# The state space's gate projection by halves of the features, four first halves taken during the scan

## The chip, the cores and the metric

The kernel runs on one core of one Trainium2 chip. The metric is the time of one execution on the device in microseconds (us). The kernel before takes 2056.19 us, the median of three runs (2054.28 to 2064.1). Engines have short names in the profile: PE multiplies matrices, PEld loads its weights, DVE is the vector engine, ACT the scalar engine, POOL is GpSimd, and SP issues most DMAs. A name that ends in q is that engine's queue.

## The reference, cut to what matters

Two transformer-like blocks are computed for 256 tokens of 1024 features. The change touches one place near the end, the second half of `s5_mixer` (a state space model with 64 groups):

```python
u = h @ w_in                                     # 1024 x 1024
s_r, s_i = associative_scan(...)                 # over the 256 tokens
y = einsum(s_r, c_re) - einsum(s_i, c_im) + d_skip * u
y = gelu(y)                                      # 256 tokens x 1024 features
ya, yb = split(y @ w_glu, 2)                     # w_glu is 1024 x 2048
return ya * sigmoid(yb)                          # 256 x 1024, then x = x + g1 * that
```

The last product is the gate projection. Each output feature needs all 1024 features of `y`. Everything is float32.

## The kernel before, in words

**Weights and their parts.** A weight matrix arrives as a stream of tiles of 128 x 2048 floats (1 MB each), issued on SP into four raw buffers. `Parts.split` (lines 131 to 149) cuts each tile into two parts of 128 x 1024, and each part into `hi`, a rounded copy that ACT makes (line 145), and `lo`, the remainder that DVE makes (line 146, `lo = w - hi`). There are four buffers for such parts. `Parts.get` hands out the next part, and sees that two more are split ahead of it. A part holds eight blocks of 128 x 128. `three` (lines 240 to 249) multiplies one block in three matmuls: `hi` with the high part of the activations (line 247), `hi` with the low part (line 248), `lo` with the high part (line 249), all added in one PSUM bank.

**The scan.** The features lie in eight chunks of 128. For c = 0 to 7, `rotated_inputs(c + 1)` multiplies on PE (line 1755), `scan(c)` does nine instructions and two more into the state `S` on DVE (lines 1766 to 1779), and `from_states(c)` multiplies the states on PE (lines 1790 and 1792) into a bank `c` that two values of c share. `load` issues the scan's tables on POOL's queue (line 1744), three chunks ahead. `fill` puts matrix-vector products of another layer's modulation between these steps (line 225, whose weights POOL's queue loads too, line 113, and whose ends are lines 229 to 237). `gelu` follows for each pair of chunks (ACT 1799, DVE 1800, ACT 1801, DVE 1804), and `outputs(half)` puts four chunks back into feature order (sixteen copies on ACT and DVE, line 1722) and makes their high and low parts `hh` and `hl` (ACT 1725, DVE 1726). `outputs(0)` is called at c = 5, and `outputs(1)` behind the loop.

**The gate projection.** Behind the loop, for each of eight output chunks d, `chunks8` is called for `ya` and for `yb` (one part, eight blocks, 24 matmuls each, k over all eight feature chunks), both into one bank of the pool of four that `rotated_inputs` uses as well. ACT's sigmoid (line 1852) and four further ACT and DVE instructions follow (lines 1853 to 1855, 1447, 1448).

**The order.** The text of the kernel is not the order of the engines. A planner orders each engine's instructions ahead of time: among those that it takes to be ready, the one written first goes first, and those marked with a low priority later. Each engine then works strictly in that order. An instruction may so stand ahead of others that were written before it: 24 matmuls of the first gate chunk stand between the scan's last matmuls, though they are written behind the loop.

Of the kernel before, what the change touches and what calls it, by code (L numbers as in the profile page):

```python
# [8 lines left out]
F32 = mybir.dt.float32  # L9
# [4 lines left out]
ALU = mybir.AluOpType  # L14
# [38 lines left out]
def bc(ap, dim, n):  # L53

    a = list(ap.ap)
    a.insert(dim, [0, n])
    return bass.AP(tensor=ap.tensor, offset=ap.offset, ap=a)
# [64 lines left out]
class Parts:  # L122
# [3 lines left out]
    def __init__(self, nc, stream, pool):  # L126
        self.nc, self.stream, self.pool = nc, stream, pool
        self.at, self.made, self.ready, self.whole = 0, {}, 0, set()

    def split(self, n):  # L130

        st = self.stream
        while self.ready < n:
            i, h = divmod(self.ready, 2)
            if h == 0:
                st.issue(i)
                self.raw = st.tiles.pop(i)
            w = self.raw[:, h * 1024:(h + 1) * 1024]
            if self.ready in self.whole:
                self.made[self.ready] = (w,)  # L140
                self.ready += 1
                continue
            parts = self.pool.tile([128, self.stream.width], F32, tag="w", name="parts").bitcast(F32R)
            hi, lo = parts[:, :1024], parts[:, 1024:]
            self.nc.scalar.copy(out=hi, in_=w)  # L145
            self.nc.vector.tensor_tensor(out=lo, in0=w, in1=hi.bitcast(F32), op=ALU.subtract)  # L146
            self.made[self.ready] = (hi, lo)
            self.ready += 1

# [91 lines left out]
def three(pe, o, w, j, a, k, first, last):  # L241

    sl = slice(j * 128, (j + 1) * 128)
    if len(w) == 1:
        pe.matmul(out=o, lhsT=w[0][:, sl], rhs=a[0][:, k], start=first, stop=last)
        return
    pe.matmul(out=o, lhsT=w[0][:, sl], rhs=a[0][:, k], start=first, stop=False)  # L247
    pe.matmul(out=o, lhsT=w[0][:, sl], rhs=a[1][:, k], start=False, stop=False)  # L248
    pe.matmul(out=o, lhsT=w[1][:, sl], rhs=a[0][:, k], start=False, stop=last)  # L249
# [1112 lines left out]
def second_block(tc, g, out):  # L1362
    nc, A, ws, ada = tc.nc, g.A, g.ws, g.ada
    v, s, pe = nc.vector, nc.scalar, nc.tensor
# [8 lines left out]
    def bank(name="b"):  # L1373
        return psb.tile([128, 512], F32, tag="b", name=name)

    def core_bank(name="c"):
        return psc.tile([128, 512], F32, tag="c", name=name)

    def small_bank(name="s"):
        return pss.tile([128, 512], F32, tag="s", name=name)  # L1380
# [28 lines left out]
    hh = b2.tile([128, 8, 256], F32R, name="h2h")  # L1409
    hl = b2.tile([128, 8, 256], F32R, name="h2l")  # L1410
# [57 lines left out]
    def chunks8(o, a):  # L1468

        w = ws.get()  # L1470
        for k in range(8):
            three(pe, o, w, k, a, k, k == 0, k == 7)
# [12 lines left out]
    for k in range(0, 8, 2):  # L1485
        b = bank()
# [7 lines left out]
    b = small_bank()  # L1494
# [3 lines left out]
    b = b[:, :4].rearrange("p (t n) -> p n t", t=2)  # L1498
# [81 lines left out]
    with ExitStack() as er:  # L1580
# [26 lines left out]
        for h in range(4):  # L1607
            q = rotated("q", 0 if h == 0 else None)
            k = rotated("k", 2 if h == 0 else None)
# [8 lines left out]
            b = core_bank()  # L1618
# [7 lines left out]
            st = r2.tile([128, 2, 6], F32, tag="st", name="st")  # L1626
# [17 lines left out]
            for t in range(2):  # L1644
# [3 lines left out]
                b = core_bank()  # L1648
# [3 lines left out]
                d = (slice(None), slice(4 * h, 4 * h + 4), slice(t * 128, (t + 1) * 128))  # L1652
# [35 lines left out]
    with ExitStack() as e5:  # L1688
# [70 lines left out]
        def scan(c):  # L1759
            b, m = rot.pop(c)  # L1760
            E = loaded.pop((1, c))
            Ec, Es = (E[:, i].rearrange("p q j -> p (q j)") for i in range(2))
            b3 = b.rearrange("p (i x) -> p i x", i=2)
            t1 = q5.tile([128, 2, 256], F32, tag="t1", name="t1")
            t2 = q5.tile([128, 2, 256], F32, tag="t2", name="t2")
            v.tensor_tensor(out=t1, in0=b3, in1=bc(Ec, 1, 2), op=ALU.mult)
            v.tensor_tensor(out=t2, in0=b3, in1=bc(Es, 1, 2), op=ALU.mult)
            z = q5.tile([128, 2, 256], F32, tag="z", name="z", bufs=1)
            v.tensor_tensor(out=t1[:, 0], in0=t1[:, 0], in1=t2[:, 1], op=ALU.add)
            v.tensor_tensor(out=t1[:, 1], in0=t1[:, 1], in1=t2[:, 0], op=ALU.subtract)  # L1770
            for i in range(2):
                v.tensor_tensor_scan(out=z[:, i], data0=m, data1=t1[:, i], initial=0.0, op0=ALU.mult, op1=ALU.add)
            v.tensor_tensor(out=t1, in0=z, in1=bc(Ec, 1, 2), op=ALU.mult)
            v.tensor_tensor(out=t2, in0=z, in1=bc(Es, 1, 2), op=ALU.mult)

            S = states[c % 2]
            t1q, t2q = (t.rearrange("p i (q j) -> p i q j", q=4)[:, :, :, :63] for t in (t1, t2))
            v.tensor_tensor(out=S[:, 0, :, 1:], in0=t1q[:, 0], in1=t2q[:, 1], op=ALU.subtract)
            v.tensor_tensor(out=S[:, 1, :, 1:], in0=t2q[:, 0], in1=t1q[:, 1], op=ALU.add)
            load(1, c + 3)  # L1780

        def from_states(c):
            o2, S = loaded.pop((2, c)), states[c % 2]
            CA = [o2[:, 640 * i:640 * i + 640].rearrange("p (q n) -> p q n", q=4) for i in range(2)]
            T = o2[:, 1280:].rearrange("p (q n) -> p q n", q=4)
            if c % 2 == 0:
                yb[c // 2] = core_bank()
            for q in range(4):
                yo = yb[c // 2][:, (c % 2 * 4 + q) * 64:(c % 2 * 4 + q) * 64 + 64]
                pe.matmul(out=yo, lhsT=T[:, q], rhs=U[:, 4 * c + q], start=True, stop=False)  # L1790
                for i in range(2):
                    pe.matmul(out=yo, lhsT=CA[i][:, q, 32:], rhs=S[:, i, q], start=False, stop=(i == 1))  # L1792
            load(2, c + 3)
# [26 lines left out]
        def fill(i):  # L1820
            while at[0] < FILL[i]:
                ada.part(small_bank, p5)
                at[0] += 1

        for c in range(8):
            if c < 7:
                rotated_inputs(c + 1)
            scan(c)
            fill(2 * c)
            if c % 2 == 0 and c >= 2:  # L1830
                gelu(c // 2 - 1, False)
            if c % 2 == 1 and c >= 3:
                gelu(c // 2 - 1, True)
                if c == 5:
                    outputs(0)
            from_states(c)
            fill(2 * c + 1)
        gelu(3, False)
        gelu(3, True)
# [5 lines left out]
        sc, sh = mod[:, 24:32], mod[:, 32:40]  # L1845
        early, sq, sums, then = next_norm(sc, sh)
        for d in range(8):
            b = bank()
            chunks8(b[:, :256], (hh, hl))
            chunks8(b[:, 256:], (hh, hl))  # L1850
            sg = q5.tile([128, 256], F32, tag="sg", name="sg")
            s.activation(out=sg, in_=b[:, 256:], func=ACTF.Sigmoid)
            v.tensor_tensor(out=sg, in0=b[:, :256], in1=sg, op=ALU.mult)
            v.scalar_tensor_tensor(out=xT[:, d], in0=sg, scalar=mod[:, 16 + d:17 + d], in1=xT[:, d], op0=ALU.mult, op1=ALU.add)
            s.activation(out=sq[:, d], in_=xT[:, d], func=ACTF.Square)
            then(d)
# [16 lines left out]
    b = ffn(1, early, R, between1, last1)  # L1873
# [5 lines left out]
    for t in range(2):  # L1879
        for h in range(2):  # L1880
            b = bank()
# [12 lines left out]
def tile_body(ctx, tc, A, out):  # L1894
    nc = tc.nc
    g = Ctx()
# [4 lines left out]
    st = Stream(nc, wst, NSTAGE, 2048)  # L1901
# [36 lines left out]
    for l in range(2):  # L1938
        st.add([A["ffn_up"][l, i] for i in range(22)])
        st.add([A["ffn_down"][l, i] for i in range(11)])  # L1940
        if l == 0:
            st.add([A["s5_w_in"][i] for i in range(4)])
            st.add([A["s5_glu"][i] for i in range(8)])

    pvt = cst.tile([128, A["pvec"].shape[1]], F32, name="pvt")
# [39 lines left out]
    with ExitStack() as es:  # L1985
# [7 lines left out]
        leftovers(tc, g)  # L1993
        es_mw.close()
    second_block(tc, g, out)


def host_arrays(inputs):
# [14 lines left out]
    I = {k: np.asarray(a) for k, a in inputs.items()}  # L2013
    d = {}
# [38 lines left out]
    def blocks(w, order):  # L2053

        K, N = w.shape
        t = w.reshape(K // 128, 128, N // 128, 128).transpose(2, 0, 1, 3)[order]
        return t.reshape(-1, 16, 128, 128).transpose(0, 2, 1, 3).reshape(-1, 128, 2048)
# [3 lines left out]
    d["ret_w_out"] = blocks(I["ret_w_out_2"][0], np.arange(8))  # L2061
    d["w_o"] = blocks(np.concatenate([wg, wo[512:]], axis=0), np.arange(8))
    d["s5_w_in"] = blocks(I["s5_w_in_2"][0], np.arange(8))
    d["s5_glu"] = blocks(I["s5_w_glu_2"][0], np.arange(16).reshape(2, 8).T.reshape(-1))
    d["ffn_up"] = np.stack([blocks(w, np.arange(44).reshape(2, 22).T.reshape(-1)) for w in I["ffn_w_up_2"]])
    d["ffn_down"] = np.stack([blocks(w, np.arange(8)) for w in I["ffn_w_down_2"]])

# [10 lines left out]
    c, s = np.cos(ang).astype(f), np.sin(ang).astype(f)  # L2078
# [28 lines left out]
```

## Time and profile before

| | |
|---|---|
| median of three runs | 2056.19 us |
| the profiled execution, its own time | 2056.63 us |
| its span, first to last instruction | 2054.9 us |
| PE busy | 1931.3 us (94%) |
| DVE busy | 1107.8 us (54%) |
| ACT busy | 649.8 us (32%) |
| POOL busy | 59.4 us (3%) |
| mean granted TensorE clock | 0.979 of 2.4 GHz |

The busy times are averages over stages that differ. The change lies in the stage from about 1724 us (the scan's start) to about 1850 us (the end of the gate projection). Times inside it are counted from the span's start. The granted clock is 1.00 at 2.4 GHz and 0.50 at 1.2 GHz.

### The profile page before, as it was taken

The numbers are of one execution on the slowest core, as the hardware profiler recorded it, in microseconds if no ns is written. First come the engines' busy times: TensorE is split into PE (matmuls) and PEld (weight loads), VectorE is DVE, ScalarE is ACT, GpSimd is POOL, SyncE is SP. The second block draws the span as 40 slices with busy tenths as digits, with TensorE's granted clock in tenths as the row PEclk, the third lists the DMA queues.
The fourth block names the chain that finished last, engine by engine and source line by source line (L and its number), as shares of the span: only waits on it lengthen the run. The fifth ranks groups of instructions, "written<-read, shape, count | busy, mean of one in ns | idle before, by whom it ended". The sixth has DMA issues, their size and how long they took to land. (4 is left out here: it accounts for less than half of the span.)

```text
span 2054.9 us, 28954 instructions
## 1 busy us (share of the span) xinstructions
PE 1931.3 (94%) x11162; PEld 1244.0 (61%) x11162; DVE 1107.8 (54%) x2364; ACT 649.8 (32%) x1134; POOL 59.4 (3%) x92
## 2 busy tenths in 40 slices
PE   6999989999899999999999979999999999799998
PEld 4756844333233333343333327888999999599998
DVE  3856654322122122132222228998898879869863
ACT  5455211000000000010000014445677646346542
POOL 1000010000000000000000000000101002100000
PEclk9999989999999999999999998999999999899999
DMA  8657659999999999999999994667857688655641
GB/s 335 224 199 278 243 193 413 421 421 421 421 422 421 421 421 421 421 421 401 421 421 421 421 374 156 215 230 275 284 213 257 251 290 301 237 181 189 225 182 62
DMA packets 101757, 643.40 MB, mean 313 GB/s; under 512 B 11584, under 2 KB 12880, under 8 KB 34288
## 3 DMA queue, kind: packets, MB, share of 16 engines
q1 hardware_dynamic: 94176, 613.46, 76.0%
q0 software_dynamic: 6624, 26.76, 3.8%
q8 instruction: 89, 1.46, 0.3%
q10 hardware_dynamic: 816, 1.30, 0.2%
q14 instruction: 52, 0.43, 0.1%
HBM read 626.79 MB, written 14.68 MB: 312 GB/s over the span
## 5 line engine op out<-in xcount | busy, mean ns | idle before, releaser
L914 PE MATMUL hc<-w,xe 128*64 128x512 f32 (+1 forms) x2008 | 470.5, 596 | 38.8 <-DMA w<-in_w_in_dram 38.7
L914 PEld LDWEIGHTS hc<-w,xe 128*64 128x64 f32 (+1 forms) x2008 | 144.6, 138 | 350.0 <-issue 234.7
L146 DVE TENSOR_TENSOR parts<-w,parts 128x1024 fp32r<-128x1024 f32 x238 | 289.3, 1219 | 57.1 <-ACT parts L145 55.5
L145 ACT CAST parts<-w 128x1024 fp32r<-128x1024 f32 x238 | 248.7, 1048 | 192.8 <-PE b L249 115.3
L247 PE MATMUL b<-h2h,parts 128*128 128x256 f32 x896 | 255.7, 286 | 10.3 <-ACT h2h L1725 9.1
L248 PE MATMUL b<-h2l,parts 128*128 128x256 f32 x896 | 255.7, 286 | 0.4 <-DVE h2l L1429 0.2
L249 PE MATMUL b<-h2h,parts 128*128 128x256 f32 x896 | 254.1, 284 | 0.0
L914 PE MATMUL yb<-w,hb 128*64 128x512 f32 (+1 forms) x1024 | 252.7, 603 | 0.8 <-DMA w<-in_w_out_dram 0.8
L934 DVE COPY hs<-hc 128x512 f32<-128x512 f32 x33 | 22.8, 691 | 417.4 <-PE hc L914 417.4
L247 PEld LDWEIGHTS b<-h2h,parts 128*128 128x128 f32 x896 | 170.5, 191 | 12.7 <-ACT h2h L1725 9.3
L248 PEld LDWEIGHTS b<-h2l,parts 128*128 128x128 f32 x896 | 170.5, 190 | 4.2 <-issue 1.3
L249 PEld LDWEIGHTS b<-h2h,parts 128*128 128x128 f32 x896 | 170.4, 190 | 0.2 <-issue 0.2
L932 ACT COPY hs<-hc 128x512 f32<-128x512 f32 x33 | 19.3, 585 | 437.0 <-PE hc L914 437.0
L914 PEld LDWEIGHTS yb<-w,hb 128*64 128x64 f32 (+1 forms) x1024 | 67.4, 138 | 129.5 <-issue 118.6
L199 DVE SCALAR_TENSOR_TENSOR acc<-w,c,acc 128x1024 f32<-128x1024 f32 x77 | 98.4, 1278 | 19.4 <-DMA w<-in_ada_w_dram 19.4
L247 PE MATMUL b<-ah,parts 128*128 128x256 f32 x352 | 100.3, 285 | 1.9 <-DVE xT L264 1.7
L249 PE MATMUL b<-ah,parts 128*128 128x256 f32 x352 | 99.8, 283 | 0.1
L248 PE MATMUL b<-al,parts 128*128 128x256 f32 x352 | 99.1, 282 | 0.0
L977 ACT COPY ys<-yb 64x512 f32<-64x512 f32 (+1 forms) x32 | 18.5, 579 | 236.1 <-PE yb L914 224.6
L896 PEld LDWEIGHTS gb<-S,h 128*128 128x128 f32 x544 | 66.5, 197 | 37.2 <-issue 26.6
L1527 PE MATMUL b<-parts,h2h 128*128 128x512 f32 x256 | 82.4, 401 | 0.9 <-DVE parts L146 0.6
L1005 DVE TENSOR_TENSOR yacc<-sc,yacc 128x512 f32<-128x512 f32 x68 | 46.6, 688 | 66.8 <-PE sc L1003 66.8
(517 smaller groups left out, 2971.6 us busy)
## 6 DMA issues: line engine op xcount, KB each, us to landing
w<-in_w_in_dram SPq DMA_DIRECT2D x252, 1024.0 KB, 19.8
w<-in_w_out_dram SPq DMA_DIRECT2D x128, 1024.0 KB, 19.8
w<-in_ffn_up_dram SPq DMA_DIRECT2D x44, 1024.0 KB, 4.9
w<-in_ada_w_dram SPq DMA_DIRECT2D x72, 512.0 KB, 5.2
w<-in_ret_w_in_dram SPq DMA_DIRECT2D x24, 1024.0 KB, 5.0
w<-in_ffn_down_dram SPq DMA_DIRECT2D x22, 1024.0 KB, 4.8
w<-in_w_ada_dram SPq DMA_DIRECT2D x32, 512.0 KB, 3.9
w<-in_ada_w_dram POOLq DMA_DIRECT2D x24, 512.0 KB, 4.7
```

Source lines behind the costliest of these rows:

```text
L145: self.nc.scalar.copy(out=hi, in_=w)
L146: self.nc.vector.tensor_tensor(out=lo, in0=w, in1=hi.bitcast(F32), op=ALU.subtract)
L199: v.scalar_tensor_tensor(out=self.acc, in0=w, scalar=cc, in1=self.acc, op0=ALU.mult, op1=ALU.add)
L247: pe.matmul(out=o, lhsT=w[0][:, sl], rhs=a[0][:, k], start=first, stop=False)
L248: pe.matmul(out=o, lhsT=w[0][:, sl], rhs=a[1][:, k], start=False, stop=False)
L249: pe.matmul(out=o, lhsT=w[1][:, sl], rhs=a[0][:, k], start=False, stop=last)
L896: g.got = pe.matmul(out=b[:, k * 128:k * 128 + n], lhsT=g.h2[:, t, d * 128:(d + 1) * 128], rhs=S[:, t, :n], start=(t == 0), stop=(t == 1))
L914: g.got = pe.matmul(out=on, lhsT=x, rhs=w[:, n * 512:n * 512 + 512], start=first, stop=last)
L932: s.copy(out=h, in_=hc[e][n])
L934: v.tensor_copy(out=h, in_=hc[e][n])
L1005: v.tensor_tensor(out=y, in0=b, in1=y, op=ALU.add)
L1527: pe.matmul(out=bs[t], lhsT=x[:, kk, tsl], rhs=y[:, k * 512:(k + 1) * 512], start=(kk == 0 and i == 0), stop=(kk == 7 and i == 2))
```

## The change

Each part of the gate's weights now holds, for one output chunk, the blocks of four feature chunks for `ya` and `yb` (2 x 4 blocks in place of 1 x 8). `glu_half(d, h)` multiplies one such part, 24 matmuls, into the bank of chunk d. The first halves (h = 0, features 0 to 511, those of `outputs(0)`) of d = 0 to 3 are written into the loop at c = 6 and 7, one behind `scan(c)` and one behind `from_states(c)`. The second halves of these, and both halves of d = 4 to 7, stay behind the loop. The host arranges the weights in that order. The `lo` of the first four gate parts is made on POOL in place of DVE.

```diff
+        self.other = set()
...
-            self.nc.vector.tensor_tensor(out=lo, in0=w, in1=hi.bitcast(F32), op=ALU.subtract)
+            (self.nc.gpsimd if self.ready in self.other else self.nc.vector).tensor_tensor(out=lo, in0=w, in1=hi.bitcast(F32), op=ALU.subtract)
...
+        def glu_half(d, h):
+
+            if h == 0:
+                glu.append(bank())
+            b, w = glu[d], ws.get()
+            for k in range(4):
+                for j in range(2):
+                    three(pe, b[:, j * 256:(j + 1) * 256], w, 2 * k + j, (hh, hl), 4 * h + k, h == k == j == 0, h == 1 and k == 3 and j == 1)
+
         for c in range(8):
             if c < 7:
                 rotated_inputs(c + 1)
             scan(c)
+            if c >= 6:
+                glu_half(2 * c - 12, 0)
             fill(2 * c)
...
             from_states(c)
+            if c >= 6:
+                glu_half(2 * c - 11, 0)
             fill(2 * c + 1)
         gelu(3, False)
         gelu(3, True)
         outputs(1)
...
         for d in range(8):
-            b = bank()
-            chunks8(b[:, :256], (hh, hl))
-            chunks8(b[:, 256:], (hh, hl))
+            if d >= 4:
+                glu_half(d, 0)
+            glu_half(d, 1)
+            b = glu[d]
...
             st.add([A["s5_w_in"][i] for i in range(4)])
+            g.ws.other |= set(range(2 * len(st.sources), 2 * len(st.sources) + 4))
             st.add([A["s5_glu"][i] for i in range(8)])
```

## Rows read from the trace of the kernel before

**Rows 1.** Busy time of each engine by stretch: length, engines, clock, DMA share, GB/s.
```profile
core 0: us, PE busy (x) PEld busy (x) DVE busy (x) ACT busy (x) POOL busy (x), PEclk, DMA share, GB/s
1740.00:1750.00 10.00, 9.33 (x85) 9.22 (x84) 10.00 (x22) 2.03 (x4) 3.60 (x7) 1.00 0.94 350
1766.00:1780.00 14.00, 13.75 (x81) 8.53 (x80) 12.29 (x24) 2.88 (x5) 1.65 (x4) 1.00 0.61 190
1782.00:1787.10 5.10, 4.95 (x22) 4.76 (x22) 1.59 (x2) 0.08 (x1) 1.00 (x2) 0.50 0.64 215
1787.10:1796.10 9.00, 0.02 (x1) 0.02 (x1) 7.98 (x14) 6.97 (x12) 1.15 (x3) 0.50 0.52 171
1796.10:1802.00 5.90, 5.90 (x26) 5.67 (x27) 5.90 (x12) 1.49 (x2) 1.58 (x3) 0.51 0.52 174
1833.00:1850.00 17.00, 17.00 (x147) 17.00 (x146) 10.46 (x14) 9.19 (x15) 0.00 (x0) 1.00 0.44 163
```

**Rows 2.** Chain of waits, scan's end: start, duration, what.
```profile
1781.64 0.34 DVE S L1778
...
1787.02 0.61 ACT g L1799
...
1795.40 0.63 ACT h2h L1725
```

**Rows 3.** PE in order of time: start, duration, what, idle before and its releaser.
```profile
1767.45 0.48 PE L247 MATMUL b<-h2h,parts 128*128 128x256 f32 x2
...
1778.90 0.28 PE L249 MATMUL b<-h2h,parts 128*128 128x256 f32 x1
...
1782.03 1.11 PE L1792 MATMUL c<-S,s5i 128*128 128x64 f32 x4 [1.89 <-DVE S L1778]
...
1796.08 0.80 PE L247 MATMUL b<-h2h,parts 128*128 128x256 f32 x2 [9.10 <-ACT h2h L1725]
```

**Rows 4.** Line 247 alone, 1766 to 1796 us (columns as in Rows 1, PE and PEld).
```profile
1766.00:1796.00 30.00, 2.16 (x8) 1.44 (x8) 0.76 0.62 206
```

**Rows 5.** ACT in order of time, gate projection: two sigmoids that follow each other.
```profile
1841.68 0.39 ACT L1852 ACTIVATE sg<-b 128x256 f32<-128x256 f32 x1 [1.75 <-PE b L249]
...
1847.82 0.38 ACT L1852 ACTIVATE sg<-b 128x256 f32<-128x256 f32 x1 [1.76 <-PE b L249]
```

**Rows 6.** DVE's waits in the scan: engine, line, for whom; us in total, times, longest.
```profile
DVE mod L235 <- PE s L232: 2.2, 2, 1.7
DVE t L1766 <- PE b L1755: 1.1, 1, 1.1
DVE g L1800 <- ACT g L1799: 0.7, 1, 0.7
```

**Rows 7.** DVE in order of time: line 146 in the scan.
```profile
1724.52 1.22 DVE L146 TENSOR_TENSOR parts<-w,parts 128x1024 fp32r<-128x1024 f32 x1
...
1728.24 1.20 DVE L146 TENSOR_TENSOR parts<-w,parts 128x1024 fp32r<-128x1024 f32 x1
...
1776.67 1.20 DVE L146 TENSOR_TENSOR parts<-w,parts 128x1024 fp32r<-128x1024 f32 x1
```

**Rows 8.** ACT in order of time: casts of the first and fourth gate part.
```profile
1720.42 1.05 ACT L145 CAST parts<-w 128x1024 fp32r<-128x1024 f32 x1
...
1730.15 1.05 ACT L145 CAST parts<-w 128x1024 fp32r<-128x1024 f32 x1
```

**Rows 9.** POOL's subtraction elsewhere, in order of time.
```profile
258.93 4.93 POOL L722 TENSOR_TENSOR h<-h,shifts 128x512 f32<-128x512 f32 x4 [252.68 <-ACT h L721]
```

**Rows 10.** DVE beside and behind Rows 9, in order of time.
```profile
260.14 2.53 DVE L746 TENSOR_SCALAR sel<-iota,fx 128x32 f32<-128x32 f32 x2
...
267.38 0.19 DVE L759 TENSOR_SCALAR rk<-rk 128x64 f32<-128x64 f32 x1
```

**Rows 11.** Waits of the POOL and SP queues from 1690 us on (columns as in Rows 6).
```profile
POOL w L113 <- PE s L225: 19.8, 6, 5.4
...
SPq L113 <- DVE parts L146: 164.9, 16, 51.7
```

More of the change, by code (lines that the diff above doesn't have):

```diff
@@ L1823, in fill @@
                 at[0] += 1
+        glu = []
+        def glu_half(d, h):
[5 more added lines that the diff above has]
+                    three(pe, b[:, j * 256:(j + 1) * 256], w, 2 * k + j, (hh, hl), 4 * h + k, h == k == j == 0, h == 1 and k == 3 and j == 1)
         for c in range(8):
@@ L2063, in host_arrays @@
     d["s5_w_in"] = blocks(I["s5_w_in_2"][0], np.arange(8))
-    d["s5_glu"] = blocks(I["s5_w_glu_2"][0], np.arange(16).reshape(2, 8).T.reshape(-1))
+    gw = I["s5_w_glu_2"][0].reshape(2, 4, 128, 2, 8, 128).transpose(4, 0, 1, 3, 2, 5).reshape(8, 2, 8, 128, 128)
+    gw = np.concatenate([gw[:4, 0], gw[:4, 1], gw[4:].reshape(8, 8, 128, 128)])
+    d["s5_glu"] = gw.reshape(8, 16, 128, 128).transpose(0, 2, 1, 3).reshape(8, 128, 2048)
     d["ffn_up"] = np.stack([blocks(w, np.arange(44).reshape(2, 22).T.reshape(-1)) for w in I["ffn_w_up_2"]])
```

## The prediction

> **What bounds the kernel now.** I read the busy times by stretch first, then the chain of waits, then PE, ACT and DVE in order of time. Up to about 1780 us the scan keeps two engines full: from 1740 to 1750 us DVE is busy 10.00 of 10 us, and from 1766 to 1780 us PE 13.75 of 14 [rows 1]. Then PE runs dry. It waits 1.89 us for the state of `scan(7)`, multiplies it from 1782.03 us on, and waits 9.10 us, until 1796.08, for the first `hh` of `outputs(1)` [rows 3]. The chain of waits runs through exactly this: DVE's state, the matmuls of `from_states(7)`, ACT's gelu at 1787.02, the copies, and ACT's cast at 1795.40 [rows 2]. From there PE is full again, 17.00 of 17 us [rows 1], so what moves the start of the second halves, or takes matmuls out of the stretch behind it, moves the end.
>
> The clock shows beside it: 0.50 granted (1.2 GHz) while the last states are multiplied and through the dry stretch, and 0.51 for the first 5.9 us behind it, then 1.00 [rows 1]. PE had done next to nothing in between: 0.02 us in 9.
>
> **What is moved and what it is worth.** The counts do not change: 384 gate matmuls, 16 parts, 16 casts, 8 weight DMAs of 1 MB. One thing is easily missed: line 247 has 8 matmuls already between 1766 and 1796 us [rows 4], and the gate's matmuls there run from 1767.45 to 1778.90 [rows 3]. With lines 248 and 249 that is 24, the first half of d = 0. So the planner takes one of the four halves now, as many as it can: with whole chunks, the next one needs a fresh bank and two more parts, with only four buffers of them. The change adds three halves, 72 matmuls, not four.
>
> Their price: two sigmoids that follow each other are 1847.82 - 1841.68 = 6.14 us apart [rows 5]; that is 48 matmuls and about 0.4 us of four small ones, so 5.74 / 2 = 2.87 us for a half at 2.4 GHz. Three halves: 8.6 us out of the full stretch. PE's two idle stretches, 1.89 + 9.10 us [rows 3], have room for them.
>
> **What it costs ahead of `hh`.** Four terms.
>
> (a) POOL's subtractions. No row shows one of 128x1024. Line 722 takes 4.93 us for four of 128x512 [rows 9], so 1.23 each, and 2.5 us for the double (an estimate from that row). DVE loses three of 1.2 us in the scan, at 1724.52, 1728.24 and 1776.67 [rows 7], 3.6 us of work; the fourth stood in a pause. But the same stretch shows what POOL does to DVE: two tiny instructions of line 746 take 2.53 us together while POOL subtracts, where a comparable one of twice the size takes 0.19 us with POOL idle [rows 10]. Each stands for as long as one POOL instruction. So the bounds are -3.6 (POOL disturbs nothing) and 4 x 2.5 - 3.6 = +6.4 us (each blocks DVE throughout). The casts of these parts run from 1720.42 to 1731.20 [rows 8]: the first subtraction falls into DVE's wait of 1.1 us for line 1755 [rows 6] and beside DVE instructions that read PSUM, the second half so, the third and fourth into the full scan. I take 0 + 1.2 + 2.5 + 2.5 - 3.6 = +2.6, nearest to rows 10. DVE later stands 1.7 us for the modulation's line 232 [rows 6], which does not move with the scan; 1.0 of it is swallowed. So the last state comes 1.6 us later, at 1783.6.
>
> The Trainium skill bears on this, in "SBUF — State Buffer", section "Who interferes with whom": a DVE instruction with two SBUF inputs contends with a GpSimd one that reads SBUF, and the later one blocks fully. Rows 10 agree with such a block, though for another kind of DVE instruction; no row shows it for the scan's. By the rule without exceptions the term would be +6.4, which is the second rival below.
>
> (b) PE ahead of `from_states(7)`. Up to 1779.5 us PE has no room, so the halves of d = 1 and 2, which are written ahead of `from_states(7)`, fall behind that: 1779.5 + 2 x 2.87 = 1785.2. That is later than the state (1783.6), and the matmuls of `from_states(7)` start there, not at 1782.03. In return PE did not pause, and I expect them at 2.4 GHz: 2.5 us in place of 5.0. They end at 1787.7, where before it was 1787.0: +0.7. Bounds: -0.9 if the planner puts d = 2 behind them (1783.6 + 2.5), and +3.2 if the clock is low all the same.
>
> (c) Splits of the second halves. The casts and subtractions of parts five and six are written ahead of the last gelu; DVE and ACT have pauses there (ACT is busy 0.08 of 5.10 us at 1782 [rows 1]). 0; 1.2 without that cover, one subtraction in the chain.
>
> (d) SP's queue waited up to 51.7 us for a line 146 [rows 11], the late one at 1776.67. With that one made at about 1734 us, 1 MB of gate weights is loaded in a stretch where the DMA engines are 0.94 busy at 350 GB/s [rows 1]: up to 2.9 us later for the scan's tables behind it. They are loaded three chunks ahead. I take 0; the bound is 2.9.
>
> **Behind `hh`.** The half of d = 3 ends by 1791, PE pauses some 6 us, so I expect the low clock at the restart as before: no gain there. In the steady gate projection DVE is busy 10.46 of 17.00 us [rows 1], 3.78 per chunk of 6.14, of which two splits are 2.45 and the rest 1.33. For the second halves alone it needs 1.22 + 1.33 = 2.55 us in each 2.87: full, with the modulation's products and `hl` of line 1726 still to do, as DVE is busy 5.90 of 5.90 us after the restart [rows 1]. Bounds 0 and +3.8 (three such splits late, 3 x 1.2, rounded up by a small one); I take +1.0, since the low clock gives DVE 5.9 us for the first 26 matmuls.
>
> **Sum.** -8.6 + 0.7 + 1.0 = -6.9 us. Against the profiled execution: 2056.63 - 6.9 = 2049.7. That execution is 0.44 us above the median of the runs, so the two count as the same.
>
> **Rivals.**
>
> 1. More than the halves. POOL disturbs DVE little, the last state is not late, d = 2 stands behind `from_states(7)`. For it: DVE is full in the scan and loses 3.6 us of work. Against: rows 10. The 1.7 us wait for line 232 limits what a faster scan gains to that. -8.6 - 2.5 (clock) - 1.0 (scan) + 0.5 = -11.6: 2045.0.
>
> 2. The lock eats it. Each subtraction blocks DVE throughout, +6.4, less 1.7 us of pause: the state comes at 1787.0, `from_states(7)` ends at 1789.5, +2.5, and +1.5 behind `hh`: -4.6, 2052.0.
>
> 3. The other side: PE stands in its fixed order for a part that POOL has not made. If the planner puts the third and fourth subtraction behind modulation loads of POOL's queue, they wait for line 225, up to 5.4 us each and 19.8 in six [rows 11]. PE, with d = 2 in front, then holds back `from_states(7)`: two such waits and 2.5 us are 13.3 us, less 8.6: +4.7, 2061.3. It decides once `hh` comes more than 8.6 us later. Against it: the casts are done by 1731.2 [rows 8], ahead of most of these loads.
>
> 4. The order stays. The planner leaves the three halves behind `hh`, or their parts are late: 2056.6. Against it: it took the first half unasked [rows 4].
>
> **How the numbers follow.** Forecast (2049.7, own range 2046.5 to 2053) 0.52; rival 1 0.16, rival 2 0.16, rival 3 0.10, rival 4 0.06. The range 2044 to 2059 leaves out part of rivals 1 and 3. About 0.5% (10.3 us) is what a measurement of this kernel can tell from no change: faster means below 2045.9, most of rival 1 and a little of the forecast's edge, 0.17; slower means above 2066.5, the worse part of rival 3, 0.05; 0.78 between.
>
> **What would show it.** 96 gate matmuls ahead of the restart in place of 24. `from_states(7)` starting near 1785 at a clock of 1.00 (b). Four POOL subtractions of about 2.5 us between 1721 and 1735, and scan instructions beside them longer than 0.7 us (a). The restart near 1797, 0.51 for some 6 us, and the last sigmoid some 7 us earlier than before. The forecast is wrong if the restart comes after 1801, if the subtractions stand past 1740, or if PE waits for parts behind the restart by more than 3 us.

## The result and the profile after

The kernel after the change takes 2068.07 us, the median of five runs (2065.59 to 2071.83), against 2056.19 us of the kernel before on the same chip (five runs, 2048.86 to 2064.1). The ratio is 1.0062, with an interval of [1.0034, 1.009]: slower, by a little more than the 0.5% that I took as the least that can be told, and outside my range. The profiled execution took 2071.83 us with a span of 2070.1 us. That is 15.2 us more than the span of before, and 3.8 us above the median of the runs.

The page gives a first hint: PE is busy 1948.5 us in place of 1931.3, with the same 11162 instructions. PE does the same work and needs 17 us longer for it.

The busy times by stretch of the kernel after (columns as in [rows 1]):

```profile
1732.00:1740.00 8.00, 8.00 (x38) 8.00 (x39) 4.39 (x11) 5.93 (x9) 0.92 (x2) 0.50 0.53 195
1740.00:1750.00 10.00, 10.00 (x41) 8.18 (x42) 8.62 (x17) 0.80 (x2) 1.25 (x2) 0.50 0.34 120
1750.00:1760.00 10.00, 8.26 (x40) 8.07 (x39) 4.76 (x10) 1.50 (x3) 2.34 (x4) 0.50 0.35 134
1760.00:1770.00 10.00, 10.00 (x48) 10.00 (x49) 6.42 (x13) 0.52 (x2) 2.28 (x4) 0.50 0.87 307
...
1774.00:1780.00 6.00, 6.00 (x30) 3.09 (x29) 5.97 (x13) 4.11 (x7) 1.08 (x2) 0.80 0.25 60
```

Compare 1740 to 1750 us with [rows 1]. There the clock was 1.00, PE got through 85 records and DVE was full. Here the granted clock is 0.50, which is 1.2 GHz, PE is full with 41 records, and DVE has time left. From about 1732 to 1776 us the scan hangs on PE instead of DVE. PE in order of time shows where this begins (start, duration, what, idle before and its releaser):

```profile
1728.19 1.89 PE L1757 MATMUL b<-U,s5i 128*128 128x64 f32 x16
1729.91 0.39 PE L1792 MATMUL c<-U,s5i 128*128 128x64 f32 x2
1731.93 1.03 PE L1794 MATMUL c<-S,s5i 128*128 128x64 f32 x4 [1.62 <-DVE S L1780]
...
1736.59 3.62 PE L1757 MATMUL b<-U,s5i 128*128 128x64 f32 x16
```

PE waits 1.62 us for the first state, and from the next matmul on everything takes twice as long: 16 records of line 1757 take 3.62 us after 1.89 before. In the kernel before PE had other work at this place (PE, in order of time):

```profile
1731.19 0.39 PE L1790 MATMUL c<-U,s5i 128*128 128x64 f32 x2
1731.42 1.95 PE L1755 MATMUL b<-U,s5i 128*128 128x64 f32 x16
1733.30 1.02 PE L225 MATMUL s<-w,c 128*1 128x512 f32 x2
1734.46 0.67 PE L1792 MATMUL c<-S,s5i 128*128 128x64 f32 x4
```

So the order has changed. With the remainders taken off DVE, the planner puts the first state ahead of DVE's copies, and PE's matmuls on it right behind line 1792's first two. The state is not late against the kernel before (1731.36 us against 1733.89); it is late against the new order. Why it is stands on POOL and DVE, in order of time:

```profile
1723.45 4.75 POOL L148 TENSOR_TENSOR parts<-w,parts 128x1024 fp32r<-128x1024 f32 x2
...
1795.87 5.60 POOL L148 TENSOR_TENSOR parts<-w,parts 128x1024 fp32r<-128x1024 f32 x2
```

```profile
1722.64 0.69 DVE L1768 TENSOR_TENSOR t<-b,s5e 128x512 f32<-128x512 f32 x1 [2.63 <-PE b L1757]
1723.24 0.68 DVE L1769 TENSOR_TENSOR t<-b,s5e 128x512 f32<-128x512 f32 x1
1723.96 4.52 DVE L1771 TENSOR_TENSOR t<-t,t 128x256 f32<-128x256 f32 x1
1728.40 0.41 DVE L1772 TENSOR_TENSOR t<-t,t 128x256 f32<-128x256 f32 x1
```

Lines 1771 and 1772 do the same kind of work on the same sizes. The first, issued 0.5 us after POOL's first subtraction, stands until POOL's second one is over: 4.52 us in place of 0.41. Line 1769, which reads one input from PSUM, is not touched (0.68).

The end of the scan and the restart, from DVE, ACT and PE in order of time:

```profile
1804.34 0.41 DVE L1780 TENSOR_TENSOR S<-t,t 128x252 f32<-128x252 f32 x1
...
1814.17 1.28 DVE L201 SCALAR_TENSOR_TENSOR acc<-w,c,acc 128x1024 f32<-128x1024 f32 x1 [1.94 <-DMA w<-in_ada_w_dram]
1815.37 0.68 DVE L1806 TENSOR_TENSOR y<-c,g 128x512 f32<-128x512 f32 x1
```

```profile
1809.21 0.60 ACT L1801 ACTIVATE g<-c 128x512 f32<-128x512 f32 x1 [1.53 <-PE c L1794]
...
1863.62 0.38 ACT L1870 ACTIVATE sg<-b 128x256 f32<-128x256 f32 x1 [1.75 <-PE b L251]
```

```profile
1806.26 0.29 PE L251 MATMUL b<-h2h,parts 128*128 128x256 f32 x1
1806.38 0.33 PE L1792 MATMUL c<-U,s5i 128*128 128x64 f32 x2
1806.55 0.61 PE L1794 MATMUL c<-S,s5i 128*128 128x64 f32 x4
...
1822.02 1.22 PE L249 MATMUL b<-h2h,parts 128*128 128x256 f32 x4 [9.60 <-ACT h2h L1727]
```

The second pair of POOL's subtractions holds DVE as well: line 1774 takes 3.39 us for two (1.26 elsewhere) and a line 148 of DVE 3.31 (1.22 elsewhere), 4.2 us in all from 1795.93 us on.

Against before, in the two profiled executions: the last state (line 1780, before 1778) comes at 1804.34 in place of 1781.64 [rows 2], 22.7 us late. The last gelu starts at 1809.21 in place of 1787.02, 22.2 late. The restart is at 1822.02 in place of 1796.08 [rows 3], 25.9 late. The last sigmoid is at 1863.62 in place of 1847.82 [rows 5], 15.8 late. So the stretch behind the restart is 10.1 us shorter; the scan had lost more than twice that. (The scan's start itself differs from execution to execution: DVE's first instruction of it comes at 1723.92 us before and at 1722.64 after.)

### The profile page after: what moved, and what is told of

Read it like the earlier page. It is cut to its first block, busy times and chain, and to the rows that moved or that the text cites. A ratio compares the mean times of both kernels' runs of the same rounds, so it can differ in the third digit from the quotient of the medians.

```text
span 2070.1 us, 28949 instructions
## 1 busy us (share of the span) xinstructions
PE 1948.5 (94%) x11162; PEld 1258.2 (61%) x11162; DVE 1112.1 (54%) x2360; ACT 649.5 (31%) x1134; POOL 69.6 (3%) x96
```

## The experiments

Each run is compared with the kernel before on the same chip (medians 2053.9 to 2055.0 us). The kernel after ran on a further chip only (before: 2056.19), so differences in us to its 2068.07 hold to about 2 us, as far as the medians of the kernel before differ; the ratios are the safer figures. My theory, A: POOL holds one DVE instruction, PE runs dry for 1.6 us, its clock falls, and the scan pays for that. B: the moved order itself (halves, banks, parts) delays the scan. "Lock only": the delay is DVE's held time and no more.

**The halves without POOL.** One line removed, so that DVE makes every remainder:

```diff
-            g.ws.other |= set(range(2 * len(st.sources), 2 * len(st.sources) + 4))
```

> The change without POOL: the halves as in the change, all remainders made on DVE. Theory A (POOL's two subtractions hold a scan instruction of DVE for 4.5 us, PE runs dry beside it, its clock falls to 1.2 GHz and stays there, and the scan becomes bound by the slow PE): the granted clock is 1.00 through the scan, the last state comes within 3 us of 1782 us, the gate projection restarts near 1797 in place of 1822, and the time is 2046 to 2052 us. Theory B (the early halves stand in PE's fixed order ahead of what the scan needs): the last state stays later than 1795, and the time is 2062 to 2070 us.

Measured: 2051.89 us (2045.85 to 2057.81), ratio 0.9982 [0.9966, 0.9999]. B falls: the halves alone make the kernel slightly faster, if anything. But 0.2% is less than the 6.9 us that I had forecast, and the executions spread over 12 us. The median is within A's range. The profiled execution, the slowest of them (2057.81), is not as A said: the last state comes at 1789.4 us and the restart at 1807.1. It shows PE dry at another place, and the clock with it (PE, then the stretches):

```profile
1743.81 3.65 PE L1757 MATMUL b<-U,s5i 128*128 128x64 f32 x16 [1.51 <-DMA s5i<-s_scratch]
```

```profile
1740.00:1750.00 10.00, 8.49 (x50) 8.38 (x50) 9.94 (x20) 2.03 (x4) 1.96 (x4) 0.68 0.83 302
1750.00:1760.00 10.00, 10.00 (x36) 6.72 (x35) 4.05 (x9) 0.40 (x1) 2.27 (x4) 0.50 0.54 188
```

**POOL without the halves.** The kernel before, with its first four gate remainders on POOL (and `split` as in the change):

```diff
+            g.ws.other |= set(range(2 * len(st.sources), 2 * len(st.sources) + 4))
```

> The kernel before with only the first four gate remainders moved to POOL; the gate projection whole, as before. Theory A: DVE's scan instruction of chunk 0 is held for 2 to 5 us, the clock is 0.50 for 30 to 50 us of the scan, and the time is 18 to 24 us above the kernel before, 2074 to 2080, since nothing is won back behind the restart. Theory A without the clock (only the lock costs): 4 to 9 us above, 2060 to 2065. Theory B: within 3 us of the kernel before.

Measured: 2070.07 us (2066.82 to 2071.29), ratio 1.0073 [1.0056, 1.0091], some 15.7 us more than before. A's size was a little too large, the rivals far too small. Its trace has the new order, the hold of 4.52 us and a wait of 1.63 us for the first state, and the clock falls without any moved half:

```profile
1732.00:1740.00 8.00, 8.00 (x32) 6.17 (x32) 7.05 (x15) 0.58 (x2) 1.25 (x2) 0.50 0.53 188
...
1760.00:1770.00 10.00, 10.00 (x35) 6.72 (x35) 3.41 (x8) 2.05 (x4) 0.00 (x0) 0.50 0.27 104
```

**A delay without POOL.** The kernel before, in which the first scan instruction of chunk 0 is issued eight times in place of once (the same values again):

```diff
-            for i in range(2):
+            for i in [0] * (8 if c == 0 else 1) + [1]:
                 v.tensor_tensor_scan(out=z[:, i], data0=m, data1=t1[:, i], ...)
```

> The kernel before, no POOL, with the first scan instruction of chunk 0 issued eight times in place of once (7 x 0.63 us = 4.4 us more on DVE; the values stay the same). Theory A: any delay of the first state by some 4 us makes PE run dry there, so the clock falls to 0.50 for tens of us and the time is 15 to 24 us above the kernel before. If it takes POOL itself, or the clock fell for another reason: 2 to 5 us above, the clock stays 1.00.

Measured: 2074.97 us (2069.37 to 2081.67), ratio 1.0096 [1.0074, 1.0117]. Seven more instructions of about 0.6 us cost some 20 us. The clock goes the same way (PE, then the stretches; the profiled execution is the slowest, 2081.67):

```profile
1736.15 0.43 PE L1790 MATMUL c<-U,s5i 128*128 128x64 f32 x2 [0.99 <-DMA s5i<-s_scratch]
1737.49 7.06 PE L1755 MATMUL b<-U,s5i 128*128 128x64 f32 x32 [0.91 <-DMA s5i<-s_scratch]
```

```profile
1740.00:1750.00 10.00, 10.00 (x49) 10.00 (x48) 9.44 (x19) 0.80 (x2) 1.78 (x3) 0.50 0.41 131
1750.00:1760.00 10.00, 10.00 (x42) 8.17 (x41) 0.00 (x0) 0.00 (x0) 1.78 (x3) 0.50 0.50 170
```

So the harm does not take POOL: a DVE delay of this length at this place can do it. The way there is not the same, though. The planner had the eight instructions to order and put later chunks' matmuls in front of the late state, and PE stood 0.99 and 0.91 us for two of the scan's tables, not for the state.

**PE kept busy over the gap.** The kernel after, with five idle 128x512 matmuls into a bank that nobody reads, behind the second chunk's rotated inputs (`g.rl` is the last matmul of these):

```diff
             scan(c)
+            if c == 0:
+                db = core_bank()
+                with tc.issue_after(g.rl.ins):
+                    for _ in range(5):
+                        pe.matmul(out=db, lhsT=g.ident, rhs=xT[:, 0:2].rearrange("p a t -> p (a t)"), start=True, stop=True)
```

> The change as it is, POOL included, plus five matmuls of 128x512 into a bank that nobody reads, on PE behind the second chunk's rotated inputs, where PE ran dry. Theory A: DVE is still held for 4.5 us, but the clock stays 1.00 in the scan; the last state comes 7 to 10 us later than in the kernel before (both pairs of POOL's subtractions) in place of 23, and the time is 2054 to 2060. If the clock is not what costs the 23 us: within 3 us of the change, 2065 to 2071.

Measured: 2060.02 us (2055.39 to 2067.44), ratio 1.0028 [1.0013, 1.0043]: 7 to 8 us less than the kernel after, with PE given 4.51 us of useless work and DVE held just as long (4.52 us). The first fall is gone. A second one came at the next state:

```profile
1726.01 4.51 PE L1846 MATMUL c<-xT,ident 128*128 128x512 f32 x10
...
1736.54 0.67 PE L1794 MATMUL c<-S,s5i 128*128 128x64 f32 x4 [1.39 <-DVE S L1780]
```

**Only the late pair on POOL.** The kernel after, with POOL making the third and fourth remainder alone:

```diff
-            g.ws.other |= set(range(2 * len(st.sources), 2 * len(st.sources) + 4))
+            g.ws.other |= set(range(2 * len(st.sources) + 2, 2 * len(st.sources) + 4))
```

> The change with only the third and fourth remainder on POOL, the first two on DVE. Theory: the scan's start is undisturbed, so no fall of the clock by POOL there; the two late subtractions hold DVE for 3 to 5 us near the scan's last chunk, as they did in the change (4.2 us on two instructions). The time is 2 to 6 us above e1: 2054 to 2058. If the third and fourth are what made the change slow: 2064 or more. If POOL's late pair is hidden: within 1.5 us of e1.

Measured: 2052.09 us (2042.27 to 2057.07), ratio 0.999 [0.9973, 1.0006], beside 2051.89 for the halves without POOL. I expected more. The hold is there all the same, near the scan's end (DVE):

```profile
1774.19 4.90 DVE L1771 TENSOR_TENSOR t<-t,t 128x256 f32<-128x256 f32 x1
```

PE has halves to multiply at that time and its clock stays at 1.00 from 1770 to 1790 us. A hold of 4.5 us costs some 16 us where PE has nothing else to do (2068.07 against 2052.09), and one of 4.9 us, where it has, costs less than the two intervals can tell, some 5 us.

This run settles one thing more. Its start of the scan has the new order without the hold, and PE does not wait there (PE):

```profile
1727.69 1.89 PE L1757 MATMUL b<-U,s5i 128*128 128x64 f32 x16
1729.42 0.39 PE L1792 MATMUL c<-U,s5i 128*128 128x64 f32 x2
1729.64 0.61 PE L1794 MATMUL c<-S,s5i 128*128 128x64 f32 x4
```

So the order alone does not bring the wait of 1.62 us; it takes the hold.

**Idle matmuls at three places.** The kernel after with the five above, three more of the same kind behind the third chunk's rotated inputs, and two behind the states of the second chunk.

> The changed kernel with POOL's four subtractions, and idle 128x512 matmuls at three places of the scan: five behind the second chunk's rotated inputs, three behind the third's, two behind the states of the second chunk. Theory (POOL's hold costs by PE's clock alone, beyond the 3 to 4 us that DVE loses): no 0.50 between 1724 and 1760, last state at 1785 to 1790, median 2050 to 2055. Rival (the hold delays the scan's chain whatever the clock is): last state past 1795, median 2058 to 2063, no better than with the five matmuls alone (2060.0).

Measured: 2055.5 us (2049.84 to 2061.39), ratio 1.0001 [0.9986, 1.0015]: 12.6 us less than the kernel after. In its trace the clock is 1.00 from 1716 to 1780 us. The median lies just above what the theory asked, and the last state is at 1791.7, later than the 1785 to 1790 that I wrote. The late pair fell on a state this time, and PE waited for it (DVE, PE):

```profile
1776.19 5.28 DVE L1780 TENSOR_TENSOR S<-t,t 128x252 f32<-128x252 f32 x1
```

```profile
1781.53 1.12 PE L1794 MATMUL c<-S,s5i 128*128 128x64 f32 x4 [3.63 <-DVE S L1780]
```

So idle matmuls alone bring back 12.6 us. The halves without POOL are 16.2 us below the kernel after (2068.07 - 2051.89). But the pair behind the second chunk's states may help without POOL too: the run with that pair and every remainder on DVE (2046.46, below) is 21.6 us below. So the clock is more than half of POOL's price, and 3.6 to 9.0 us of it remain with the clock held until the late pair. DVE stands 9.0 us in the two holds of this trace (4.52 + 5.28 - 2 x 0.41), and the eight further idle matmuls take PE's time; these runs do not part the two.

**What keeps the halves from their worth.** The next three start from the halves without POOL. First, the scan's first tables in four buffers, loaded one chunk earlier:

```diff
-                t = q5.tile([128, b - a], F32, tag=f"s5i{what}", name="s5i", bufs=3)
+                t = q5.tile([128, b - a], F32, tag=f"s5i{what}", name="s5i", bufs=4 if what == 0 else 3)
...
-            load(0, c + 3)
+            load(0, c + 4)
...
+        load(0, 3)
```

> The halves without POOL (as e1), and the scan's first tables (512 KB each, read by the rotated inputs) held in four buffers in place of three, each loaded one chunk earlier. Theory: in e1's profile PE waits 1.51 us for such a table at 1743.8 us, its clock then falls to 0.50 for 15 us, and DVE waits 9.5 us; with the table earlier that wait is gone, the clock stays 1.00 through the scan, and the time is 2043 to 2048 us, 4 to 8 below e1's median of 2051.9. Rival: the DMA engines are full there (share 0.83 to 1.01 in e1 from 1716 to 1750), so the earlier table only moves the wait to another table; 2049 to 2054.

Second, in place of that, eight idle 128x512 matmuls behind the last states, to hold the clock up to the restart:

> The halves without POOL (as e1), and eight matmuls of 128x512 into a bank that nobody reads, on PE behind the last states, where PE waits some 9 us for the gate's second halves. Theory: the gate projection restarts at 1.00 in place of 0.50, which costs 5.9 us at half speed in the kernel before, so 2 to 3 us less than e1: 2048 to 2050. Rival: the clock falls all the same, or the idle matmuls stand in front of the restart: within 1 us of e1, or above it.

Third, both:

> The earlier tables (e5) and the idle matmuls behind the last states (e6) together. Theory: both gains add, 6 to 10 us below e1: 2041 to 2046, some 10 us under the kernel before. Rival: 2047 to 2052, if one of them does nothing.

Measured: 2049.97 (2045.64 to 2055.7), ratio 0.9979 [0.9963, 0.9994]; 2053.66 (2044.2 to 2057.0), 0.9979 [0.9958, 0.9999]; 2049.44 (2044.06 to 2057.61), 0.9985 [0.9968, 1.0001]. In all three the theory misses and the rival holds, and none can be told from the halves without POOL (0.9982). In the trace of the second the clock is 1.00 at the restart (1.00 from 1790 to 1810 us), and the median did not move for it. In the first and third the wait for tables came in two parts (0.41 and 0.78 us; 0.75 and 0.82) and did not go, and the clock still fell (PE, the first of the three):

```profile
1745.43 3.67 PE L1757 MATMUL b<-U,s5i 128*128 128x64 f32 x16 [0.78 <-DMA s5i<-s_scratch]
```

The second has the scan of the halves without POOL, and its longest stop for a table from 1738 to 1760 us is 0.26 us: the 1.51 us were those of one execution. Its clock fell behind a wait of 1.49 us for modulation weights. (The DMA engines, full in the first expectation from 1716 to 1750 us, had a share of 0.66 from 1732 to 1740 in that trace.)

Then the other remedy, two idle 128x512 matmuls where PE stood for the table, behind the states of the second chunk (`g.fl` is the last matmul of these):

```diff
             from_states(c)
+            if c == 1:
+                db = core_bank()
+                with tc.issue_after(g.fl.ins):
+                    for _ in range(2):
+                        pe.matmul(out=db, lhsT=g.ident, rhs=xT[:, 0:2].rearrange("p a t -> p (a t)"), start=True, stop=True)
```

> The halves with every remainder on DVE (as in the run that leaves POOL out), and two idle 128x512 matmuls into an unread bank behind the states of the second chunk, where PE stood 1.51 us for a table of the scan and its clock then fell to 0.50 for some 16 us. Theory (the clock lost at that stop is what keeps the halves from their 8.6 us, and what spreads the executions): no 0.50 in the scan, median 2045 to 2049, a spread below 8 us. Rival (the table comes late in any case, and DVE, not PE's clock, sets the scan's length): 2050 to 2054, spread as before, 10 us or more.

Measured: 2046.46 us (2042.45 to 2051.68), ratio 0.9961 [0.9945, 0.9978], 7.5 us below the kernel before, with a spread of 9.2 us (the theory said below 8, the rival 10 or more). This is the lowest median that ran, beside the last version below; its interval and that of the halves without POOL (0.9982 [0.9966, 0.9999]) still overlap. PE in its trace stands for only 0.68 us there, and the group after it runs on at 2.4 GHz:

```profile
1739.92 1.94 PE L1856 MATMUL c<-xT,ident 128*128 128x512 f32 x4
1742.53 0.41 PE L1757 MATMUL b<-U,s5i 128*128 128x64 f32 x2 [0.68 <-DMA s5i<-s_scratch]
...
1754.41 3.56 PE L227 MATMUL s<-w,c 128*1 128x512 f32 x4 [0.59 <-DMA w<-in_ada_w_dram]
```

The last line is a small fall that stayed, against the theory's "no 0.50": four records at 3.56 us, where other such groups take 1.88. The next stretch is at 1.00 again. The same two idle matmuls in the kernel before, as a control:

> The kernel before with the same two idle matmuls behind the states of the second chunk: what they are worth by themselves. Theory: the kernel before's profiled execution shows a stop of only 0.67 us at that place and no fall of the clock, but its executions differ by 15 us; where they do because the stop is sometimes longer, the two matmuls take the slower half away: median 2049 to 2053, spread below 10 us. Rival (they only take PE's time, 1.8 us, in a stretch where DVE is full): 2053 to 2056, spread as before.

Measured: 2053.72 us (2051.88 to 2060.84), ratio 0.9993 [0.9976, 1.0009]. By themselves they are worth nothing there that can be told; the rival holds for the median, and the spread (9.0 us) is as the theory said.

**The wait in front of the last copies.** In the version with two idle matmuls (2046.46) DVE stands in a new place between the last state and the copies, and ACT and PE behind it:

```profile
1790.31 0.68 DVE L1806 TENSOR_TENSOR y<-c,g 128x512 f32<-128x512 f32 x1
1794.44 1.28 DVE L201 SCALAR_TENSOR_TENSOR acc<-w,c,acc 128x1024 f32<-128x1024 f32 x1 [3.44 <-DMA w<-in_ada_w_dram]
1795.64 3.17 DVE L1724 COPY uT<-y 32x256 f32<-32x256 f32 x8
```

Line 201 is a modulation product that is written behind `outputs(1)` at low priority; the planner put it in front, and its weights are late. In the kernel after it is the 1.94 us shown above. I held these products, with their loads, until the last copy:

```diff
-        ada_step(4)
+        ada_step(4, g.oc.ins)
```

> The kernel with the halves, every remainder on DVE and two idle matmuls in the scan (2046.5), and the modulation's products that are written behind outputs(1) (lines 199 and 201, with their weight loads) held until its last copy. Theory (DVE stands 3.4 to 4.2 us for modulation weights in front of the last copies, which takes back that much of the halves): from the last state to the restart 14 to 14.5 us in place of 17.8, median 2042 to 2045. Rival (the products and their loads only move behind the restart, where DVE is full, and hold up the sigmoids' chain): the restart comes 3 us earlier, but the median stays at 2045.5 to 2048.

Measured: 2047.3 us (2044.21 to 2051.5), ratio 0.9956 [0.9935, 0.9977]. From the last gelu to the restart it took 1800.45 - 1790.51 = 9.94 us in place of 1799.56 - 1787.88 = 11.68, so the wait is gone, but the median did not move, as the rival said. In this execution the last state came 2.1 us later (1784.65 against 1782.56), and the first one 2.5 (1732.90 against 1730.40), so that was lost ahead of the scan. The same edit in the kernel before:

> The kernel before with the modulation's products behind outputs(1) held in the same way. Theory: there DVE's one wait for modulation weights, 1.75 us, lies in the pause between the state and the gelu, so nothing is gained in front of the copies: 2053 to 2056. Rival (the products cost before as much as after, and the halves' loss has another cause): 2049 to 2052.

Measured: 2052.47 us (2048.48 to 2062.88), ratio 0.9979 [0.996, 0.9999]. That is between theory and rival. Whether this wait is worth anything to the whole execution stays open.

## Why the prediction was wrong, step by step

**Step (a) failed, and with it the forecast.** I took POOL's subtractions at +2.6 us, 1.6 of it at the last state; measured, the last state came 22.7 us late. The duration was right (4.75 us for two, 2.4 each; I had 2.5). Two things were wrong. First, I expected DVE and POOL to alternate one for one, as in [rows 10], and priced the first subtraction at 0 because it would fall beside line 1755 and instructions that read PSUM. It did begin there, but the next DVE instruction has two SBUF inputs and stood through what was left of both, 4.52 us. With the second pair DVE stood 4.1 + 4.2 = 8.3 us longer.

The Trainium skill says of such a pair, in "SBUF — State Buffer", section "Who interferes with whom", that the one issued later blocks fully. The trace agrees, with 4.52 us for 0.41, and goes further: the instruction stood through two of POOL's, not one. My second rival took this rule without exceptions, and its bound of +6.4 us was still far too low.

Second, and by the idle matmuls this is more than half of it, I priced the delay as DVE time alone. Nothing in the sum stood for what PE does while it waits, nor for the new order that the planner makes once the remainders are off DVE. The profile before showed the pieces: a wait of 1.89 us in [rows 3] with the clock at 0.50 behind it in [rows 1]. I used that pair only at the scan's end. With 0.50 in the scan, PE's 128x64 matmuls no longer fit beside DVE's work, PE becomes the bound, and the state is 22.7 us late. That the clock is the larger part is shown from two sides: POOL's delay with PE kept busy costs 12.6 us less, and a hold as long over a busy PE costs nothing that can be told from the spread. A DVE delay without POOL, which ends in the same low clock by another wait, costs as much (+20).

The Trainium skill speaks of this, in "TensorE: Matmul & The Clock Gate", section "HAM oscillation — how this bites in real kernels": waits between stretches of work send the array back to its half clock, and the change of clock is paid again each time. I had not weighed it against the change. The trace agrees that a wait is followed by 0.50, though this one, 1.62 us, is shorter than those of that section's example; the some 44 us at 0.50 that came behind it, with PE at work, are this trace's own.

**Step (b)** was right. PE is still at the halves when the state is ready (1804.34 + 0.41 = 1804.75 us), and `from_states(7)` begins right behind them, at 1806.38, 1.6 us later; I had 1783.6 to 1785.2, 1.6 as well. It ran at 2.4 GHz, 0.61 us for four records in place of 1.11. From state to gelu it is 0.5 us less than before; the +0.7 of my sum holds a state 1.6 us late, so I had 0.9 less.

**Step (c)** was too small: 0, with a bound of 1.2. From the last gelu to the restart the kernel after takes 12.81 us, before 9.06. Of the 3.7 us more, one split (1.22 us, at 1810.41 on DVE) stands in the chain, as my bound had it. The rest is modulation products in front of line 1802 and of line 1806, the second late by 1.94 us for its weights; the sum had no term for these. The run that holds the products back takes 1.7 us less for this stretch than its fellow in the trace (9.94 against 11.68), without a gain in the median.

**Step (d)** is not shown either way. A table was late by 1.51 us in one execution of the halves, by 0.67 in the profile before; no run shows that the gate's weights made it so.

**The halves** gave what I had priced or a little more: 10.1 us from restart to last sigmoid in place of 8.6, and 9.4 in the version with two idle matmuls (1841.95 - 1799.56 = 42.39 us, before 51.74). Part of the surplus is not theirs. The kernel before has a stretch at a lower clock here that the kernel after does not have (before; in the kernel after the clock is 1.00 from 1828 us to the last sigmoid):

```profile
1826.00:1833.00 7.00, 7.00 (x50) 7.00 (x49) 2.60 (x6) 2.69 (x6) 0.00 (x0) 0.76 0.26 83
```

That is 3.4 us at half speed, some 1.7 us of work. The +1.0 that I added behind `hh` did not come. All 96 matmuls of the first halves do stand ahead of the restart, so rival 4 falls too.

**The rivals.** Rival 1 falls with (a). Rival 2 saw the lock and not the clock. Rival 3 had the sign and not the cause: POOL's second pair was indeed planned behind modulation loads, at 1795.87, past the 1740 that I had named as a sign of error, but PE waits at most 0.22 us between 1780 us and the end of the halves at 1812; the 9.60 us behind that are for `hh`. (In the sum of rival 2 the state comes at 1786.7, not 1787.0; nothing hangs on it.) My forecast of -6.9 us is near the -7.5 of the version with two idle matmuls (2046.46 against 2053.92). That version has no subtraction on POOL, so the nearness is luck. The change itself, with PE's dry spells covered, only comes back to the kernel before (1.0001).

## What to carry to other kernels

When a change delays one engine, look at what PE has to do in that time: here one of 4 us that left PE dry among small matmuls cost some 16, and one over a full PE nothing that could be told. An instruction moved to GpSimd is not free for DVE: look at which DVE instructions with two SBUF inputs stand beside it, and at the order that the planner makes of the move. A few idle matmuls in front of a short, known wait are a cheap test of whether the clock is what is lost; here they gave back more than half.

## What the runs showed of the hardware

A fall could last long with PE at work. Behind 1.62 us the clock stayed at 0.50 for some 44 us, through groups of 128x64 matmuls with PE busy 8 to 10 of 10 us, and it was back after a group of line 227 (128x512, four records from 1773.57 us on). In the version with two idle matmuls it was back behind one such group, 3.56 us.

The length of the dry spell alone does not say whether the clock falls: 1.39, 1.51, 1.62, 1.89 and 3.63 us were each followed by 0.50; 0.67 us in the kernel before and 0.68 us were not, and 0.59 and 0.78 us were. The executions differ in what ran before as well, so no rule is drawn from this.

Executions of one kernel differ by 9 to 15 us in most of these runs, and those of the kernel before by 14 to 22 us on each chip. That this is the clock, falling in some executions and not in others, would fit the smaller spread of the version with two idle matmuls (9.2 us) and of the control (9.0 us), but the control's median is that of the kernel before, and only one execution of each kernel has a trace. It stays open.
